# Pools that wait per tile, and three stages moved in a two-layer mixer, attention and FFN kernel (Trainium2, one core)

## The chip, the cores and the metric

The kernel runs on one core of a Trainium2 chip. The metric is the device time of one execution in microseconds (us). The engines are TensorE (PE, with PEld for its weight loads), VectorE (DVE), ScalarE (ACT), GpSimd (POOL) and SyncE (SP, which here only issues transfers).

## The reference

Two residual layers on x of 2048 positions by 1024 features, float32:

```
block 1:  h = x @ w_in;  y = concat(SGU(h), conv module(h), HGRN2(h)), each times silu(gate)
          x1 = layernorm(sqrt(2)*x + y @ w_out)
block 2:  n = rmsnorm(x1); y = concat(attention heads on n, a pooling mixer on n)
          x2 = x1 + y @ w_out2
          m = rmsnorm(x2);  x3 = x2 + (act(m @ w_gate) * (m @ w_up)) @ w_down
out = rmsnorm(x3)
```

The FFN is 1024 to 2816 to 1024. Positions are the rows; attention is causal.

## The kernel before

Every float32 operand is split into an fp16 high and an fp16 low part, and a product is three matmuls (high x high, high x low, low x high). The kernel runs its stages one after the other in the program, and a scheduler of the framework then sets, ahead of time, the order of the instructions of each engine; each engine works through its own list in that order. A transfer is issued by the engine in whose list it stands, almost always SP.

SBUF and PSUM are handed out by pools (`pool`, L71). A pool that is opened where an earlier one has been closed lies in its space, and the first write into the new pool waits until all tiles of the old pool that it lies on are released, pool against pool.

- **Block 1** ends with `out_phase` (L550): the mixers' output y lies in a DRAM scratch y1d, written by `store` (L194) as 512-position rows, loaded for 256 positions at a time (L567), multiplied by w_out, normalized, transposed by DMA.
- **Block 2** (`block2`, L705) runs six attention units, each in four blocks of 512 positions, in pools named E (10 tiles, `e`), U and others. Scores are matmuls into `sc` (L831), the exponentials are cast on POOL and ACT (L844, L845), transposed by DMA on SP (`e<-e`, L847) and multiplied with v (`po`, L868). `store` writes each unit's output to the scratch y2d. The pooling mixer runs between attention rows.
- **Second projection** (`out2`, L621): opens after block 2's pools close. One pool `gen` of eight 4 KB buffers (per partition) holds three of the eight w_out2 row weights (made on ACT, L120, and POOL, L121; the other five go to the always open pool W) and the y tiles: four tiles of 256 positions are needed for a pair of steps, and five buffers are left for them. For eight steps u of 2 x 128 positions: y loads (L650), x1 load (L657), 2 x 2 groups of 24 matmuls into `pq` (L663 to L665), the add (L666), the store of x2 (L667), Square (L671), scaling (L673), seven sums for a Strassen-like product (`seven`), fp16 splits (L680, L681), and DMA transposes on SP (L692, 11 for a step) into T7 tiles in the pools x7 and T (`th`, `tl`).
- **FFN, first part** (`ffn_in`, L1079): 22 blocks of 128 hidden features in pairs, each for two halves of the positions. A product is 7 sub-products of 12 matmuls (L1102 to L1104). Each pair's weights come by `seven_weights` (L1056, L1057 loads into the two-buffer pool WS; L1063 to L1066 on POOL; L1069 casts on ACT; L1070 low parts on DVE or POOL). The hidden values go to a DRAM scratch `md` (L1153).
- **FFN, second part** (`ffn_out`, L1157): opens its own pools `wd`, `gwt`, `gm`, `gs`, `gsm` where `ffn_in`'s have closed, loads all eight x2 rows (L1168), makes three sets of w_down weights (a set is two loads, four POOL operations, three ACT casts, three DVE subtractions), and multiplies the `mid` tiles (L1240) with them (L1190 to L1192), in four chunks of 3, 3, 3 and 2 pairs; the accumulation goes back into the x2 rows (L1184, L1198, L1200), and `finish` normalizes and stores.

Of the kernel before, what the change touches and what calls it, by code (L numbers as in the profile page):

```python
# [7 lines left out]
F32 = mybir.dt.float32  # L8
F16 = mybir.dt.float16
# [9 lines left out]
D = 1024  # L19
# [47 lines left out]
class Kernel:  # L67
# [3 lines left out]
    def pool(self, name, bufs=1, space=None, ctx=None):  # L71
        kw = {"space": space} if space is not None else {}
        return (ctx or self.ctx).enter_context(self.tc.tile_pool(name=name, bufs=bufs, **kw))
# [115 lines left out]
    def y_scratch(self, name):  # L189
        return [  # L190
            [self.dram.tile([128, KD, 512], F16, name=f"{name}{b}{p}") for p in "hl"] for b in range(NB)
        ]

    def store(self, yd, k, b, src, scale=None):  # L194
# [10 lines left out]
        nc.sync.dma_start(yd[b][0][:, k], yh)  # L205
        nc.sync.dma_start(yd[b][1][:, k], yl)
# [336 lines left out]
    def out_phase(self, cw, blk):  # L543
# [19 lines left out]
        for b in range(NT // 2):  # L563
            y = []
            for p in range(2):
                t = yp.tile([128, KD, 256], F16, tag=f"y{p}", name="y")
                nc.sync.dma_start(t, yd[b // 2][p][:, :, (b % 2) * 256:(b % 2 + 1) * 256])  # L567
                y.append(t)
            yh, yl = y
            for c in range(2):  # L570
                t = b * 2 + c
                cs, ts = slice(c * 128, (c + 1) * 128), slice(t * 128, (t + 1) * 128)
# [8 lines left out]
                for n in range(2):  # L581
                    ns = slice(n * 512, (n + 1) * 512)
                    ps = pq()
                    for k in range(KD):
                        wh, wl = w[k]
                        nc.tensor.matmul(ps, yh[:, k, cs], wh[:, ns], start=k == 0, stop=False)
                        nc.tensor.matmul(ps, yh[:, k, cs], wl[:, ns], start=False, stop=False)
                        nc.tensor.matmul(ps, yl[:, k, cs], wh[:, ns], start=False, stop=k == KD - 1)
# [33 lines left out]
    def out2(self, cw):  # L622
# [20 lines left out]
        for u in range(4 * NB // 2):  # L643
            half, tp = u // 4, u % 4
            if tp % 2 == 0:
                ys = []
                for q in range(2):
                    for p in range(2):
                        t = gen.tile([128, KD, 256], F16, tag="w", name="y")
                        nc.sync.dma_start(t, self.y2d[2 * half + q][p][:, :, tp * 128:tp * 128 + 256])  # L650
                        ys.append(t)
            xs = []
            cs = slice(tp % 2 * 128, tp % 2 * 128 + 128)
            for q in range(2):
                yh, yl = ys[2 * q:2 * q + 2]
                r = m.tile([128, D], F32, tag="x2", name="x2")
                nc.sync.dma_start(r, self.x1d[8 * half + 4 * q + tp])  # L657
                for n in range(2):
                    ns = slice(n * 512, (n + 1) * 512)
                    ps = pq()  # L660
                    for k in range(KD):
                        wh, wl = w[k]
                        nc.tensor.matmul(ps, yh[:, k, cs], wh[:, ns], start=k == 0, stop=False)  # L663
                        nc.tensor.matmul(ps, yh[:, k, cs], wl[:, ns], start=False, stop=False)  # L664
                        nc.tensor.matmul(ps, yl[:, k, cs], wh[:, ns], start=False, stop=k == KD - 1)  # L665
                    nc.vector.tensor_tensor(r[:, ns], r[:, ns], ps, ALU.add)  # L666
                nc.sync.dma_start(self.x2d[u][:, q], r)  # L667
                xn = xp.tile([128, 2, 512], F32, tag="xn", name="xn")
                xf = xn.rearrange("p h n -> p (h n)")
                ss = sm.tile([128, 1], F32, tag="ss", name="ss")  # L670
# [670 lines left out]
```

## Time and profile before

| what | value |
|---|---|
| median of 3 runs (lowest to highest) | 3462.16 us (3456.29 to 3462.77) |
| profiled execution, its own time | 3461.33 us |
| its span in the trace | 3459.5 us |
| PE busy | 3128.8 us (90%), 17736 matmuls |
| DVE busy | 2270.6 us (66%) |
| POOL busy | 1337.9 us (39%) |
| ACT busy | 1217.1 us (35%) |

PE is the engine that is busiest throughout. A stretch in which its busy time or its granted clock (PEclk, 1.00 being full speed, 2.4 GHz) is low is one in which it waits or has just waited. In time order: block 1 to 957 us, attention to 1968, second projection 1978 to 2177, FFN first part to 3003, second part to the end.

### The profile page before, as it was taken

Reading aid. Unit: us, or ns where it says so; the run is one execution under the profiler, and the core shown is the slowest. Engines: PE = TensorE matmul, PEld = TensorE weight load, DVE = VectorE, ACT = ScalarE, POOL = GpSimd, SP = SyncE. Lnnn points to the kernel's source line nnn. Section 1 sums busy time; section 2 is a strip of 40 time slices with the busy share of each in tenths; the row PEclk is TensorE's granted clock in tenths of the full one; section 3 lists DMA queues with packets and bytes.
Section 4 is the critical chain, followed back from the end, with each engine's and each line's share of the span. In section 5 each row is a group of like instructions: output and inputs, shape, how many; then the busy total and the mean of one; then the engine's idle time right before and its main releaser. Section 6 shows DMA issues by size and latency. Waiting matters only on the chain. (4 is left out here: it accounts for less than half of the span.)

```text
span 3459.5 us, 46900 instructions
## 1 busy us (share of the span) xinstructions
PE 3128.8 (90%) x17736; PEld 1586.8 (46%) x17736; DVE 2270.6 (66%) x3661; ACT 1217.1 (35%) x2259; POOL 1337.9 (39%) x1181
## 2 busy tenths in 40 slices
PE   8999998999987799868789698999999999789998
PEld 4454454784444455434444343344444444334443
DVE  6986878525648888889785644555655656454436
ACT  5223232322234466644565522332322332221103
POOL 5344354404335544474553400333322232074325
PEclk9999999999998999989999798999999999899999
DMA  5101011216756666546545677422222222533334
GB/s 186 37 17 46 13 50 50 63 32 193 182 139 120 126 124 139 117 102 126 123 100 112 141 176 198 115 67 80 79 83 67 81 83 80 209 129 133 112 109 161
DMA packets 575106, 371.84 MB, mean 107 GB/s; under 512 B 434848, under 2 KB 524704, under 8 KB 573856
## 3 DMA queue, kind: packets, MB, share of 16 engines
q1 hardware_dynamic: 567360, 348.22, 38.9%
q10 hardware_dynamic: 7520, 20.63, 1.7%
q8 instruction: 139, 2.28, 0.3%
q14 instruction: 87, 0.71, 0.1%
HBM read 162.70 MB, written 82.31 MB: 71 GB/s over the span
## 5 line engine op out<-in xcount | busy, mean ns | idle before, releaser
L142 PE MATMUL pg<-th,w 128*128 128x512 f16 x1344 | 522.4, 389 | 39.3 <-DVE r L590 11.8
L144 PE MATMUL pg<-th,w 128*128 128x512 f16 x1344 | 522.2, 389 | 5.9 <-POOL w L155 3.0
L143 PE MATMUL pg<-tl,w 128*128 128x512 f16 x1344 | 522.6, 389 | 0.7 <-DVE tl L181 0.7
L868 PE MATMUL po<-v,e 128*128 128x128 f16 (+1 forms) x1088 | 170.6, 260 | 107.9 <-DMA e<-e 91.2
L980 POOL TENSOR_TENSOR e<-e 128x128 f32<-128x128 f32 (+7 forms) x96 | 165.1, 1723 | 193.7 <-DVE e L974 154.6
L845 POOL TENSOR_TENSOR e<-e 128x1024 f16<-128x1024 f32 (+4 forms) x96 | 154.8, 1627 | 196.5 <-ACT e L844 165.3
L844 ACT CAST e<-e 128x1024 f16<-128x1024 f32 (+7 forms) x192 | 150.4, 794 | 222.8 <-POOL e L967 98.0
L143 PEld LDWEIGHTS <-w 128*128 128x128 f16 x1344 | 134.4, 100 | 182.9 <-issue 46.3
L142 PEld LDWEIGHTS <-w 128*128 128x128 f16 x1344 | 134.5, 100 | 171.0 <-issue 17.5
L144 PEld LDWEIGHTS <-w 128*128 128x128 f16 x1344 | 134.1, 100 | 166.4 <-issue 15.5
L974 DVE TENSOR_TENSOR_SCAN e<-e,few 128x129 f32<-128x129 f32 (+7 forms) x96 | 185.4, 1936 | 34.7 <-POOL e L967 31.4
L1070 POOL TENSOR_TENSOR w<-ws,w 128x1024 f16<-128x1024 f32 x20 | 48.0, 2400 | 393.3 <-ACT w L1069 393.3
L831 PE MATMUL sc<-k,q 128*128 128x512 f16 (+2 forms) x480 | 173.8, 364 | 28.1 <-DVE e L894 22.2
L465 DVE SCALAR_TENSOR_TENSOR acc<-h,cols,acc 128x512 f32<-128x512 f32 x240 | 193.5, 826 | 2.4
L1103 PEld LDWEIGHTS <-w 128*128 128x128 f16 x1232 | 120.7, 98 | 161.6 <-issue 20.5
L1102 PEld LDWEIGHTS <-w 128*128 128x128 f16 x1232 | 120.7, 98 | 150.7 <-ACT w L1069 4.8
L1104 PEld LDWEIGHTS <-w 128*128 128x128 f16 x1232 | 120.7, 98 | 149.6 <-DVE w L1070 4.0
L899 ACT ACTIVATE e<-e,nm 128x1024 f32<-128x1024 f32 (+4 forms) x192 | 171.2, 893 | 51.0 <-DVE e L894 25.8
L832 PE MATMUL sc<-k,q 128*128 128x512 f16 (+2 forms) x480 | 172.2, 366 | 0.0
L868 PEld LDWEIGHTS <-e 128*128 128x128 f16 x1088 | 107.9, 104 | 136.9 <-issue 59.4
L869 PE MATMUL po<-v,e 128*128 128x64 f16 (+1 forms) x1088 | 163.8, 216 | 0.0
L121 POOL TENSOR_TENSOR w<-ws,w 128x1024 f16<-128x1024 f32 x52 | 117.9, 2270 | 113.3 <-ACT w L120 113.2
(317 smaller groups left out, 8000.2 us busy)
## 6 DMA issues: line engine op xcount, KB each, us to landing
mid<-md SPq DMA_DIRECT2D x88, 448.0 KB, 4.2
ws<-in_w SPq DMA_DIRECT2D x48, 512.0 KB, 3.8
md<-mid SPq DMA_DIRECT2D x44, 512.0 KB, 3.4
md<-mid SPq DMA_DIRECT2D x22, 768.0 KB, 5.7
q<-qn SPq DMA_DIRECT2D x96, 128.0 KB, 2.4
ws<-in_wg SPq DMA_DIRECT2D x22, 512.0 KB, 3.5
ws<-in_wu SPq DMA_DIRECT2D x22, 512.0 KB, 4.1
ws<-in_wd SPq DMA_DIRECT2D x22, 512.0 KB, 3.8
```

Of the source, the lines that this page charges most:

```text
L142: nc.tensor.matmul(ps, wh[:, k], th[:, k], start=k == 0, stop=False)
L143: nc.tensor.matmul(ps, wh[:, k], tl[:, k], start=False, stop=False)
L144: nc.tensor.matmul(ps, wl[:, k], th[:, k], start=False, stop=k == KD - 1)
L465: nc.vector.scalar_tensor_tensor(acc[:, ct], src, wcol, acc[:, ct], ALU.mult, ALU.add)
L831: nc.tensor.matmul(ps[:, 0:n], q[:, 0], kk, start=True, stop=False)
L832: nc.tensor.matmul(ps[:, 0:n], q[:, 1], kk, start=False, stop=not last)
L845: eng.tensor_tensor(fv[:, n:2 * n], A[:, 0:n], fv[:, 0:n], ALU.subtract)
L868: nc.tensor.matmul(po, t[:, 0, j], v, start=x == 0, stop=False)
L869: nc.tensor.matmul(po[:, 0], t[:, 1, j], v[:, 0], start=False, stop=x == len(todo) - 1)
L899: nc.scalar.activation(e[r][:, 0:n], e[r][:, 0:n], AF.Exp, bias=nm[:, len(sc) - 1:len(sc)], scale=-1.0, accum_out=ss[:, r, x:x + 1])
L974: nc.vector.tensor_tensor_scan(rev, rev, self.zero.to_broadcast([128, n + 1]), 1.0, ALU.mult, ALU.add)
L980: nc.gpsimd.tensor_tensor(A[:, 0:n], g[:, 1:n + 1], g[:, 0:n], ALU.subtract)
```

## The change

1. All SBUF and PSUM pools get `reuse_waits="tile"`: a tile of a new pool waits only for the tiles of the old pool that it lies on. A pool can be put on the right side of SBUF; x7 is.
2. The y scratches are laid out in blocks of 128 positions. A load of y is then one contiguous piece for each partition (4 KB in `out_phase`, 2 KB in `out2`; before, 512 B pieces), and a store is four pieces of 256 B for each partition (before, one of 1 KB).
3. `out2`: the w_out2 weights and the y tiles have pools of their own, `gen` with 3 buffers and `uy` with eight 2 KB buffers; y is loaded for 128 positions at a time (32 loads of 256 KB in place of 16 of 512 KB). The pools are opened in another order. The normalized row is written in place; Square goes by halves into a PSUM tile, and one more POOL addition joins the two sums (16 more instructions on ACT and on POOL in all). The x1 rows have 5 buffers instead of 2.
4. FFN: the pools for w_down's intermediate sums, `seven`'s sums and the mid tiles are opened once for both parts. The first three w_down sets are made in the last gate/up pair, between its gate and its up product. An x2 row is asked for one step ahead, instead of all eight at the start. The extra mid pool has one buffer, used in one turn of six (before two, in two turns of seven).

```diff
     def pool(self, name, bufs=1, space=None, ctx=None, side="left"):
         kw = {"space": space} if space is not None else {}
+        if space is not DRAM:
+            kw |= {"reuse_waits": "tile", "side": side}
...
-            [self.dram.tile([128, KD, 512], F16, name=f"{name}{b}{p}") for p in "hl"] for b in range(NB)
+            [self.dram.tile([128, 4, KD, 128], F16, name=f"{name}{b}{p}") for p in "hl"] for b in range(NB)
...
-        nc.sync.dma_start(yd[b][0][:, k], yh)
-        nc.sync.dma_start(yd[b][1][:, k], yl)
+        for p, t in enumerate((yh, yl)):
+            nc.sync.dma_start(yd[b][p][:, :, k], t.rearrange("p (c t) -> p c t", c=4))
...
-                t = yp.tile([128, KD, 256], F16, tag=f"y{p}", name="y")
-                nc.sync.dma_start(t, yd[b // 2][p][:, :, (b % 2) * 256:(b % 2 + 1) * 256])
+                t = yp.tile([128, 2, KD, 128], F16, tag=f"y{p}", name="y")
+                nc.sync.dma_start(t, yd[b // 2][p][:, b % 2 * 2:b % 2 * 2 + 2])
...
-        gen = self.pool("gen", 8, ctx=cw)
-        xp = self.pool("ux", 2, ctx=cw)
+        sm = self.pool("usm", 4, ctx=cw)
+        gen = self.pool("gen", 3, ctx=cw)
+        yp = self.pool("uy", 8, ctx=cw)
+        m = self.pool("um", 5, ctx=cw)
+        hp = self.pool("uh", 5, ctx=cw)
         sp = self.pool("us", 1, ctx=cw)
-        hp = self.pool("uh", 5, ctx=cw)
-        m = self.pool("um", 2, ctx=cw)
-        sm = self.pool("usm", 4, ctx=cw)
         pq = self.banks("upq", UPQ, cw)
+        jp = self.pool("ujk", 1, PSUM, ctx=cw)
...
-            if tp % 2 == 0:
-                ys = []
-                for q in range(2):
-                    for p in range(2):
-                        t = gen.tile([128, KD, 256], F16, tag="w", name="y")
-                        nc.sync.dma_start(t, self.y2d[2 * half + q][p][:, :, tp * 128:tp * 128 + 256])
-                        ys.append(t)
...
+                y = []
+                for p in range(2):
+                    t = yp.tile([128, KD, 128], F16, tag="y", name="y")
+                    nc.sync.dma_start(t, self.y2d[2 * half + q][p][:, tp])
+                    y.append(t)
...
+                    nc.vector.tensor_tensor(r[:, n], r[:, n], ps, ALU.add)
+                    junk = jp.tile([128, 512], F32, tag="junk", name="junk")
+                    nc.scalar.activation(junk, r[:, n], AF.Square, accum_out=ss[:, n:n + 1])
+                nc.sync.dma_start(self.x2d[u][:, q], rf)
+                nc.gpsimd.tensor_tensor(ss[:, 0:1], ss[:, 0:1], ss[:, 1:2], ALU.add)
+                self.rstd(ss[:, 0:1], ss[:, 0:1], self.eps_rms, 1.0 / D)
+                nc.vector.scalar_tensor_tensor(rf, rf, ss[:, 0:1], gr, ALU.mult, ALU.mult)
...
-            self.x7 = self.pool("x7", 6, ctx=c3)
+            self.x7 = self.pool("x7", 6, ctx=c3, side="right")
...
+            self.wt = self.pool("fwt", 1, ctx=cw)
+            self.sp = self.pool("fs", 1, ctx=cw)
+            self.mp = self.pool("gm", 1, ctx=cw)
+            self.sm = self.pool("gsm", 4, ctx=cw)
...
                     wg = weights(a["wg"], f + 2, 0, nc.gpsimd)
+                elif half:
+                    self.sets = [self.down_weights(j, 0, j) for j in range(CHUNKS[0])]
                 proj(wu, half, h, False)
...
-        for t in range(8):
+
+        def row(t):
             r = self.tp.tile([128, 2, D], F32, tag=("th", "tl")[t % 2], name="x2")
             nc.sync.dma_start(r, self.x2d[t])
             rows.append(r)
...
-        sets = [weights(j, 0, j) for j in range(CHUNKS[0])]
+        sets = self.sets
+        row(0)
...
-                    pool, tag = (mp, "m") if turn % 7 in (2, 5) else (self.wp, "w")
+                    pool, tag = (self.mp, "m") if turn % 6 == 1 else (self.wp, "w")
...
+                if len(rows) < 8:
+                    row(tp + 1)
```

`down_weights` is the old inner function `weights` of `ffn_out` made a method.

How the lists change at three places. The number of matmuls is the same, and block 1's lists are alike but for two ACT rows.

SP's list before, at the end of the attention (`e<-e` are the transposes of the exponentials, `ws<-in_wo` the last w_out2 row, y2d0 to y2d3 the scratch by 512 positions, h and l its high and low parts):

```order
L847 DMA_TRANSPOSE e<-e 128x14x128
L205 DMA y2d2h<-yh 128x512
L206 DMA y2d2l<-yl 128x512
L847 DMA_TRANSPOSE e<-e 128x16x128 x2
L132 DMA ws<-in_wo 128x1024
L650 DMA y<-y2d0h 128x8x256
L650 DMA y<-y2d0l 128x8x256
L650 DMA y<-y2d1h 128x8x256
L650 DMA y<-y2d1l 128x8x256
L657 DMA x_18882<-x1d_7493 128x1024
```

SP's list now, some twenty transfers earlier in the attention's end:

```order
L653 DMA y<-y2d0h 128x1024
L653 DMA y<-y2d0l 128x1024
L134 DMA ws<-in_wo 128x1024
L1061 DMA ws<-in_wg 128x1024
L848 DMA_TRANSPOSE e<-e 128x16x128
L848 DMA_TRANSPOSE e<-e 128x2x128
L848 DMA_TRANSPOSE e<-e 128x16x128
L848 DMA_TRANSPOSE e<-e 128x4x128
L848 DMA_TRANSPOSE e<-e 128x16x128
L848 DMA_TRANSPOSE e<-e 128x6x128
L208 DMA y2d1h<-yh 512x1x128
L653 DMA y<-y2d1h 128x1024
```

The first two y loads, the last w_out2 row and the first gate row, which stood behind the attention's last transposes, now stand ahead of fifteen of them. The first load of y2d1 stands right behind the store that it reads, and seven more y loads follow between transposes: ten of 256 KB in all ahead of the attention's last transpose.

PE's list before, at the same place (`po` is the attention's last product, `pt` a transpose of its result, `pq` the second projection):

```order
L868 LDWEIGHTS e
L868 MATMUL po<-v,e 128x256
L869 LDWEIGHTS e
L869 MATMUL po<-v,e 128x128
L876 MATMUL pt<-ident,o_18377 128x128 x4
L663 LDWEIGHTS y
L663 MATMUL pq<-w,y 128x512
L664 LDWEIGHTS y
```

PE's list now, at the last query block's scores (`sc`):

```order
L833 LDWEIGHTS q
L833 MATMUL sc<-k_17310,q 128x384
L835 LDWEIGHTS bias_8827
L835 MATMUL sc<-bias_8827 128x128
L665 LDWEIGHTS y
L665 MATMUL pq<-w,y 128x512
L666 LDWEIGHTS y
```

Two groups of the second projection (48 matmuls) now stand among the scores of the attention's last rows, and 44 more matmuls of it around the last `po` products: about 92 of 768 that were all behind the last `po`.

PE's list before, at the passage from the FFN's first part to its second (`pa`, `pb`, `pc` are the accumulators; `th`, `tl` and `x_` tiles hold the first part's input, `mid` the second's):

```order
L1103 LDWEIGHTS w_24931
L1103 MATMUL pa<-tl,w_24931 128x512
L1104 LDWEIGHTS w_24931
L1104 MATMUL pa<-th,w_24931 128x512
L1190 LDWEIGHTS mid
L1190 MATMUL pc<-wd,mid 128x512
L1191 LDWEIGHTS mid
L1191 MATMUL pc<-wd,mid 128x512
```

PE's list now:

```order
L1107 MATMUL pc<-th,w_25164 128x512
L1108 LDWEIGHTS w_25164
L1108 MATMUL pc<-x_18864,w_25164 128x512
L1197 LDWEIGHTS mid
L1197 MATMUL pb<-wd,mid 128x512
L1198 LDWEIGHTS mid
L1198 MATMUL pb<-wd,mid 128x512
L1199 LDWEIGHTS mid
```

The first products of the second part (L1197 to L1199 of the changed kernel) stand ahead of the last 72 matmuls of the first part. SP's list there, before (`md` is the scratch of the hidden values, `x_` from x2d the x2 rows):

```order
L1168 DMA x_25584<-x2d_18857 128x2048
L1240 DMA mid<-md_20146 128x1792
L1153 DMA md_20167<-mid 512x1x512 x2
L1153 DMA md_20167<-mid 512x1x768
L1240 DMA mid<-md_20148 128x1792 x2
L1056 DMA ws<-in_wd 128x1024
L1057 DMA ws<-in_wd 128x1024
L1056 DMA ws<-in_wd 128x1024
L1057 DMA ws<-in_wd 128x1024
```

and now:

```order
L1061 DMA ws<-in_wd 128x1024
L1062 DMA ws<-in_wd 128x1024
L1248 DMA mid<-md_20232 128x1792
L1159 DMA md_20249<-mid 512x1x512 x2
L1159 DMA md_20249<-mid 512x1x768
L1061 DMA ws<-in_wd 128x1024
L1062 DMA ws<-in_wd 128x1024
L1184 DMA x_25697<-x2d_18853 128x2048
L1061 DMA ws<-in_wd 128x1024
L1062 DMA ws<-in_wd 128x1024
L1184 DMA x_25840<-x2d_18855 128x2048
L1061 DMA ws<-in_wd 128x1024
```

The loads for sets 2 and 3 of w_down stood behind the last stores into `md`; all three sets' loads, and the first of set 4, now stand ahead of the last two groups of `md` stores.

## Rows read from the trace of the kernel before

**Rows 1.** Table of stretches: length, then each engine's busy time and count, PEclk, DMA share.

```profile
1860.00:1963.00 103.00, 77.46 (x465) 43.69 (x464) 82.76 (x223) 69.94 (x142) 47.77 (x31) 0.89 0.57 119
1963.00:1978.00 15.00, 5.99 (x35) 4.20 (x32) 3.29 (x2) 5.37 (x13) 8.45 (x6) 0.61 0.41 107
1978.00:2177.00 199.00, 176.79 (x771) 77.48 (x772) 90.26 (x106) 44.37 (x61) 11.78 (x31) 0.91 0.77 192
...
2950.00:3003.00 53.00, 51.09 (x236) 22.82 (x234) 28.30 (x42) 11.80 (x20) 0.00 (x0) 1.00 0.43 153
3003.00:3052.00 49.00, 18.43 (x59) 6.54 (x58) 20.98 (x20) 13.83 (x15) 22.30 (x14) 0.69 0.60 218
3052.00:3100.00 48.00, 43.30 (x191) 19.00 (x191) 29.30 (x32) 10.26 (x10) 38.20 (x22) 0.96 0.46 154
```

**Rows 2.** PE's waits, attention's end (1860 to 1978): total us, times, longest.

```profile
PE po L868 <- DMA e<-e: 14.8, 6, 5.0
PE sc L831 <- DVE e L894: 9.3, 11, 2.6
PE pt L876 <- DVE o L948: 8.5, 1, 8.5
```

**Rows 3.** Timelines of POOL and of SP's queue around the second projection's start.

```profile
1969.59 4.64 POOL L121 TENSOR_TENSOR w<-ws,w 128x1024 f16<-128x1024 f32 x2
...
1971.73 0.34 SPq L132 DMA_DIRECT2D ws<-in_wo  x1
1972.19 0.60 SPq L650 DMA_DIRECT2D y<-y2d0h  x1
```

**Rows 4.** PE's waits in the second projection (1978 to 2177).

```profile
PE pq L665 <- DMA y<-y2d2l: 16.0, 2, 8.2
PE pq L665 <- DMA y<-y2d0l: 5.9, 2, 4.5
```

**Rows 5.** Timeline of PE behind one of those waits.

```profile
2082.86 0.61 PE L665 MATMUL pq<-w,y 128*128 128x512 f16 x1 [8.22 <-DMA y<-y2d2l]
...
2086.67 0.63 PE L665 MATMUL pq<-w,y 128*128 128x512 f16 x1
2087.10 0.45 PE L663 MATMUL pq<-w,y 128*128 128x512 f16 x1
```

**Rows 6.** PE's waits at the FFN's middle (3003 to 3100).

```profile
PE pb L1190 <- ACT wd L1069: 13.4, 3, 8.8
PE pc L1190 <- DMA mid<-md: 12.1, 1, 12.1
PE pa L1190 <- DVE x L1184: 2.4, 1, 2.4
```

**Rows 7.** Timeline of POOL: the first three w_down sets.

```profile
2929.89 1.77 POOL L1063 TENSOR_TENSOR ws<-ws 128x512 f32<-128x512 f32 x1 [0.93 <-DVE u L1125]
...
3020.26 1.26 POOL L1064 TENSOR_TENSOR wt<-ws 128x512 f32<-128x512 f32 x1 [88.60 <-DMA md<-mid]
...
3029.05 1.27 POOL L1064 TENSOR_TENSOR wt<-ws 128x512 f32<-128x512 f32 x1
...
3039.13 2.12 POOL L1064 TENSOR_TENSOR wt<-ws 128x512 f32<-128x512 f32 x1 [1.75 <-DVE wd L1070]
```

**Rows 8.** Transfers: share by queue (1978 to 2177); landing and issue times by tile.

```profile
q1 hardware_dynamic: 72957, 37.62, 75.8%
...
L692 SPq DMA_TRANSPOSE tl<-hl x32: 1210/1257/2001, 2104.6 to 2192.7; - x32
...
DMA to landing us min/median/max: 1.9/2.0/5.4
```

**Rows 9.** SP's queue at the attention's end (1860 to 1972): its longest waits.

```profile
SPq L847 <- POOL e L845: 46.0, 12, 10.4
```

**Rows 10.** The page's costliest groups: the matmuls of block 2's first products among them.

```profile
L142 PE MATMUL pg<-th,w 128*128 128x512 f16 x1344 | 522.4, 389 | 39.3 <-DVE r L590 11.8
```

More of the change, by code (lines that the diff above doesn't have):

```diff
@@ L69, in __init__, with pool @@
         self.tc, self.nc, self.a, self.out, self.ctx = tc, tc.nc, a, out, ctx
-    def pool(self, name, bufs=1, space=None, ctx=None):
+    def pool(self, name, bufs=1, space=None, ctx=None, side="left"):
         kw = {"space": space} if space is not None else {}
+        if space is not DRAM:
+            kw |= {"reuse_waits": "tile", "side": side}
         return (ctx or self.ctx).enter_context(self.tc.tile_pool(name=name, bufs=bufs, **kw))
@@ L1057, in seven_weights @@
         nc.sync.dma_start(r2, b2)
-        t = wt.tile([128, 3, 512], F32, tag="wt", name="wt")
+        t = self.wt.tile([128, 3, 512], F32, tag="wt", name="wt")
         if inner:
@@ L1155, in ffn_in, with down_weights @@
                     )
+    def down_weights(self, f, c, j):
+        if c % 2:
+            h, lo = [self.wd[j].tile([128, 7, 512], F16, tag=p, name="wd") for p in "hl"]
+        else:
+            h, lo = [self.x7.tile([128, 7, 512], F16, tag="x7", name="wd") for _ in range(2)]
+        pools = [(h[:, s], lo[:, s]) for s in (slice(0, 2), slice(2, 4), slice(4, 7))]
+        wd = self.a["wd"]
+        src = [wd[(2 * f + x) * 128:(2 * f + x + 1) * 128].rearrange("p (h n) -> p h n", h=2) for x in range(2)]
+        return self.seven_weights(*src, False, pools, self.nc.vector)
     def ffn_out(self, cw):
         nc, a = self.nc, self.a
-        wd = [self.pool(f"wd{j}", 1, ctx=cw) for j in range(max(CHUNKS))]
-        wt = self.pool("gwt", 1, ctx=cw)
-        mp = self.pool("gm", 2, ctx=cw)
-        sp = self.pool("gs", 1, ctx=cw)
-        sm = self.pool("gsm", 4, ctx=cw)
-        fg = self.bcast(sp, a["final_g"], D, "fg")
+        self.wd = [self.pool(f"wd{j}", 1, ctx=cw) for j in range(max(CHUNKS))]
+        sp, sm = self.sp, self.sm
+        fg = self.bcast(sp, a["final_g"], D, "s3")
         rows = []
-        for t in range(8):
+        def row(t):
             r = self.tp.tile([128, 2, D], F32, tag=("th", "tl")[t % 2], name="x2")
@@ L1169, in ffn_out @@
             rows.append(r)
-        def weights(f, c, j):
-            if c % 2:
-                h, lo = [wd[j].tile([128, 7, 512], F16, tag=p, name="wd") for p in "hl"]
-            else:
-                h, lo = [self.x7.tile([128, 7, 512], F16, tag="x7", name="wd") for _ in range(2)]
-            pools = [(h[:, s], lo[:, s]) for s in (slice(0, 2), slice(2, 4), slice(4, 7))]
-            src = [a["wd"][(2 * f + x) * 128:(2 * f + x + 1) * 128].rearrange("p (h n) -> p h n", h=2) for x in range(2)]
-            return self.seven_weights(*src, False, wt, pools, nc.vector)
         def down(pairs, tp):
@@ L1233, in ffn_out @@
                 if tp == 1 and c + 1 < len(CHUNKS):
-                    nxt = [weights(at + n + j, c + 1, j) for j in range(CHUNKS[c + 1])]
+                    nxt = [self.down_weights(at + n + j, c + 1, j) for j in range(CHUNKS[c + 1])]
                 pairs = []
```

44 lines of the change are left out of this document (18 added, 26 removed).

## The prediction, made before the changed kernel had run

> **What bounds the kernel now.** I first read the table of stretches [rows 1], asking in which of them PE stands still or runs at a low granted clock, and then, for those alone, PE's waits, the timelines around them, and the transfers. Where nothing disturbs it PE sets the pace: from 2950 to 3003 it is busy for 51.09 of 53 us with 236 matmuls at PEclk 1.00, that is 0.2165 us each. Against this unit four places fall off. At the end of the attention (1860 to 1963) PE is busy for 77.46 of 103 us. Between attention and second projection (1963 to 1978) it is busy for 5.99 of 15 at PEclk 0.61. In the second projection 771 matmuls take 199 us where they would need 771 x 0.2165 = 167: 32 us lost. In the middle of the FFN, 59 matmuls take 49 us and then 191 take 48: (49 - 12.8) + (48 - 41.4) = 43 us lost. The change touches just these places.
>
> **The wait between attention and second projection.** The end of a chain is seen in [rows 3]: POOL makes row weights of the second projection at 1969.59, which need space of `gen` and so the end of the attention's pools; the last weight load can go out only at 1971.73 and the first y load follows at 1972.19. PE's wait for the attention's last result (8.5 us for `pt`, [rows 2]) lies in the same stretch, but the second projection doesn't need the last query block to begin. With a wait per tile and the y loads ten transfers ahead of the attention's last transposes, PE finds ready groups there. What PE does do in the stretch is worth 5.99 x 0.61 = 3.7 us at full clock, so 15 - 3.7 = **11 us** go. Bounds: 0, if the space that the new pools lie on is released last, to 11.
>
> **Groups moved into the attention's end.** About 92 of the 768 matmuls stand earlier in PE's list: 92 x 0.2165 = 20 us. PE's idle time in the attention's end is 14.8 us for transposed exponentials and 9.3 us for DVE's exponent work [rows 2], 24 us together, so there is room. Against it: ten y loads stand on SP ahead of exponent transposes, at 0.60 us for an issue [rows 3] 6 us of queue; behind them wait the transposes, and PE's `po` for those. SP itself waits 46.0 us for POOL's casts there [rows 9], so I take half of it as hidden: 20 - 3 = **17 us**. Bounds: 20, if all is hidden, to -5, if the groups stand in PE's list before their y has landed and hold the last scores behind them, for one wait like the 5.0 us of [rows 2], while gaining nothing.
>
> **Waits for y in the second projection.** PE waits 16.0 us for y2d2 low and 5.9 for y2d0 low [rows 4]; behind each wait matmuls are 0.43 us apart (2086.67 to 2087.10) instead of 0.2165, and only then does the clock return [rows 5]. 22 us of waits and 10 of low clock make the 32. The cause is space: a pair of steps needs four y tiles of 4 KB and only five buffers are left beside three weights, so the next pair's tiles can be asked for only when the last matmuls of this pair are done. Eight buffers of 128 positions hold two steps, and one step's buffers come free every 96 matmuls = 21 us, more than a landing. I leave 10 us for one wait with its low clock and take **22 us**. Bounds: 5, if transfers are what is late and not buffers (first rival), to 31.
>
> **Smaller pieces in stores, larger in loads.** Stores into y2d landed in 2.0 us at the median, in a row that counts eight stores and two loads of y2d2's low part together [rows 8]. The new first load of y2d1 stands right behind its store and needs it to have landed; two loads are so exposed, some 2 us each, within the 3 us above. Pieces of 256 B in a store aren't in this trace; as bounds I take no change and a doubling of the 2.0 us, 4 us for the two loads. The Trainium skill, "DMA: Bandwidth & Descriptors", Specifications, speaks against this edit: it asks for at least 512 B in a transfer for line rate, below which the DMA engine does a read-modify-write. By the trace the stores cost nothing visible; by that rule, with a doubling of the landing as an estimate, the sum would be 4 us smaller, 3380. No run here shows it yet.
>
> **Block 1 to block 2, and the added instructions.** PE waits 11.8 us for `r` before block 2's first product [rows 10]. A wait per tile frees one PSUM bank an add earlier, not the normalization that it waits for: **1 us**, bounds 0 to 4. The 16 extra instructions on ACT and on POOL lie in a stretch in which these are busy for 44.37 and 11.78 of 199 us [rows 1]: nothing. If that cover were gone, POOL's extra addition would stand in each row's chain of normalization, which ends in T7 and is not waited for until the FFN starts.
>
> **The middle of the FFN.** POOL's first sum for w_down waits 88.60 us, until 3020.26, for the last store of the hidden values, because its pool lies where the first part's pools were [rows 7]; the sets follow at 3029.05 and 3039.13, 9 to 10 us apart, and PE waits 13.4 us for ACT's casts and 12.1 for a `mid` tile that stands behind eight x2 rows [rows 6]. Now the sum's pool is the same in both parts, and all three sets are made in the last pair, during whose last half POOL is busy for 0.00, ACT for 11.80 and DVE for 28.30 of 53 us [rows 1]. Three sets, 9.4 us apart, are 28 us, and they can begin at 2929.89, where POOL already worked on the first [rows 7], 73 us before 3003. So they end in time. Of the 43 us I leave 9: 2.4 us for x2 adds [rows 6], which aren't touched, and half of the 12.1 for one late `mid` tile. Gain **34 us**; bounds 18 (the `mid` wait and its low clock stay in full and one set is late) to 42.
>
> **The sum.** 11 + 17 + 22 + 1 + 34 = 85 us. The profiled execution took 3461.33 us, 0.8 below the median of 3462.16, too little to matter: 3461.3 - 85 = **3376 us**.
>
> **The rivals.** *Transfers pace the second projection.* DMA's share is 0.77 over 199 us, the highest of these stretches, 153 us of work, nearly all in SP's queue [rows 1, 8]. My forecast leaves 199 - 22 - 20 = 157 us for the stretch; the ten loads moved ahead are 2.6 of its 37.62 MB, so 142 us of work would fill 0.91 of it. If no more than 0.77 is to be had, it takes 142 / 0.77 = 184 us, 27 more: **3403**. For it: 88 transposes at 1.257 us [rows 8] are 111 us of SP alone. Against it: the y loads' pieces are four times as long, which shortens their work. The Trainium skill, "Perfetto Trace Analysis", What "DMA-bound" means, would call it bound by the issuing engine's sequencer if SP's track were solid with transfers. Chance 0.20.
>
> *The moved groups gain nothing.* They fall where PE isn't idle, or what they fill is given back behind `po`: 17 less, **3393**. Chance 0.09.
>
> *The w_down sets are late in the last half.* If WS's two buffers, shared with the last gate and up weights, keep the loads back, PE waits in front of the first products, which now stand ahead of the last 72 matmuls of the first part: the gain is 12 instead of 34, **3398**. The longest wait for ACT's cast was 8.8 us [rows 6]. Chance 0.10.
>
> *Slower: the y loads hold SP's queue.* A load waits on SP for its buffer's space in E and U, and all transposes of exponentials wait behind it, then `po`, then the release of the next E tile. SP's longest wait of this kind was 10.4 us [rows 9]. At 10.4 us for each of ten loads it is 104 us, 3376 + 104 = **3480**. It decides from 85 / 10 = 8.5 us for a load. Against it: the pools now wait for single tiles, and the list puts the loads between transposes, where E tiles come free one by one. Chance 0.11, of which 0.03 end near 3461, where the change would also be seen to do nothing.
>
> *All at its best bounds.* 11 + 20 + 31 + 4 + 42 = 108: **3353**. Chance 0.06.
>
> **How the numbers follow.** That leaves 0.44 for the forecast, whose own range is 3364 to 3390. The range for 8 in 10 goes from 3348, just under the best bounds, to 3425, the first and third rivals together (27 + 22 more); outside lie the slower case and a little at the lower end. Faster by over 0.2% (7 us, about what a measurement of this kernel can tell from no change): 0.44 + 0.20 + 0.09 + 0.10 + 0.06 = 0.89; within 0.03; slower 0.08.
>
> **What would show it.** First two steps: `pq` matmuls inside the attention's end, no stretch of PEclk 0.6 behind the last `po`, PE's waits for `e<-e` no longer than 14.8 us. Third: no wait of PE for y, and the second projection ending near 2127 instead of 2177; if it ends near 2154 with DMA near 0.77 and waits for y, the first rival holds. FFN: POOL's 88.60 us wait gone, its w_down sums before the end of the first part, and 250 matmuls in about 65 us where there were 97. It would be wrong if PE waited for y or transposes among the last scores, or for w_down before the last 72 matmuls.

## The result, and the profile after

The changed kernel takes 3414.74 us (median of 4 runs, 3411.95 to 3417.88) against 3462.47 of the kernel before in the same comparison: ratio 0.9867, 95% interval 0.9849 to 0.9884. That is 47.7 us less; the forecast was 86 less (3376). The time lies in the range 3348 to 3425, but not in the 3364 to 3390 that the prediction gave to its own forecast. The profiled execution took 3417.88 us, its span is 3416.1.

The table of stretches of the changed kernel, in the same stretches as [rows 1] (length, then busy time and count of PE, PEld, DVE, ACT and POOL, PEclk, DMA share, GB/s):

```profile
1860.00:1963.00 103.00, 86.95 (x519) 46.27 (x517) 85.01 (x219) 70.75 (x140) 56.52 (x34) 0.97 0.69 148
1963.00:1978.00 15.00, 10.98 (x88) 7.09 (x88) 3.08 (x5) 2.36 (x10) 3.76 (x4) 1.00 1.03 272
1978.00:2177.00 199.00, 169.36 (x748) 73.85 (x747) 102.32 (x118) 61.10 (x107) 36.94 (x57) 0.92 0.76 187
...
2950.00:3003.00 53.00, 44.14 (x180) 18.67 (x180) 42.37 (x48) 18.39 (x26) 15.65 (x10) 0.91 0.73 264
3003.00:3052.00 49.00, 43.51 (x187) 18.76 (x185) 28.26 (x26) 8.28 (x9) 31.74 (x18) 0.93 0.52 185
3052.00:3100.00 48.00, 48.00 (x225) 21.72 (x222) 15.12 (x22) 2.35 (x4) 14.32 (x8) 1.00 0.28 98
```

Three stretches look as forecast. PE is busy for 86.95 of 103 us in the attention's end instead of 77.46, and for 10.98 of 15 behind it at PEclk 1.00 instead of 5.99 at 0.61. In the middle of the FFN it does 187 matmuls in 49 us instead of 59. But the stretch from 1978 to 2177 still shows PEclk 0.92 with fewer matmuls than before. PE's waits from 1860 to 2200 in the changed kernel (total us, times, longest) say why, set against [rows 2, 4]:

```profile
PE pa L1106 <- ACT junk L670: 17.4, 1, 17.4
PE po L869 <- DMA e<-e: 8.2, 7, 2.5
PE sc L832 <- DVE e L895: 6.0, 10, 2.0
PE pa L1106 <- ACT s L1121: 4.5, 1, 4.5
PE pc L1106 <- ACT w L1074: 2.7, 1, 2.7
PE pq L665 <- DMA y<-y2d2h: 2.0, 2, 1.7
```

The waits for y are down from 22 to some 4 us, those for transposed exponentials from 14.8 to 8.2. A wait that didn't exist has come: 17.4 us before the FFN's first matmul, and 4.5 and 2.7 right behind it. How far ahead of the kernel before the changed kernel is, is best seen where the same matmul starts in both traces (numbers counted within each part, us in the two spans):

| matmul | before | changed | ahead |
|---|---|---|---|
| second projection, last of 768 | 2176.3 | 2122.3 | 54.0 |
| FFN first part, 49th | 2199.3 | 2167.8 | 31.5 |
| FFN first part, 3547th of 3696 | 2965.7 | 2934.3 | 31.5 |
| FFN second part, 49th of 1848 | 3043.1 | 2988.6 | 54.5 |
| FFN second part, 301st | 3108.7 | 3057.9 | 50.8 |
| FFN second part, last | 3450.0 | 3405.6 | 44.5 |

So the second projection ended 54.0 us earlier, about what the first terms say (11 + 17 + 22 + 1). The FFN's start gave 22.5 back. Its middle brought 23.0, and the second part lost 10.0 of that on the way.

Who holds PE at the FFN's start? Rows of DVE, PE and SP in the changed kernel behind the last `pq` matmul at 2122.3 (L674 is the scaling, L668 the addition that empties a `pq` bank):

```profile
2124.98 1.28 DVE L674 SCALAR_TENSOR_TENSOR x<-x,ss,ws 128x1024 f32<-128x1024 f32 x1 [8.66 <-DMA x2d<-x]
...
2138.57 0.68 DVE L668 TENSOR_TENSOR x<-x,pq 128x512 f32<-128x512 f32 x1
2146.42 2.53 DVE L674 SCALAR_TENSOR_TENSOR x<-x,ss,ws 128x1024 f32<-128x1024 f32 x2 [7.17 <-DMA x2d<-x]
...
2140.11 0.58 PE L1106 MATMUL pa<-x,w 128*128 128x512 f16 x1 [17.44 <-ACT junk L670]
...
2150.14 0.53 SPq L1062 DMA_DIRECT2D ws<-in_wg  x1
```

Until 2124.98 the scaling waits 8.66 us for `x2d<-x`, the store of the raw row, because it now overwrites that row in place. The last addition comes at 2138.57, 16 us behind the last `pq` matmul, PE's first FFN matmul at 2140.11 behind it, the last scalings at 2146.42, and only behind them the second load of the first gate row (2150.14), whose WS buffer held the broadcast norm weight. DVE's waits from 1970 to 2170 in the changed kernel:

```profile
DVE x L674 <- DMA x2d<-x: 55.7, 10, 10.0
DVE hl L682 <- DMA x<-hl: 13.9, 7, 3.3
```

55.7 us for the raw rows' stores: the kernel before has no such wait in the same part, since there the normalized row had a tile of its own.

### The profile page after: what moved, and what is told of

The parts are those of the page before. It is cut to its first block, busy times and chain, and to the rows that moved or that the text cites. A ratio compares the mean times of both kernels' runs of the same rounds, so it can differ in the third digit from the quotient of the medians.

```text
span 3416.1 us, 46957 instructions
## 1 busy us (share of the span) xinstructions
PE 3110.3 (91%) x17736; PEld 1576.9 (46%) x17736; DVE 2274.2 (67%) x3661; ACT 1217.8 (36%) x2291; POOL 1357.9 (40%) x1197
## 5 line engine op out<-in xcount | busy, mean ns | idle before, releaser
L869 PE MATMUL po<-v,e 128*128 128x128 f16 (+1 forms) x1088 | 161.4, 252 | 98.6 <-DMA e<-e 85.3
L146 PEld LDWEIGHTS <-w 128*128 128x128 f16 x1344 | 133.7, 100 | 165.8 <-issue 13.5
L870 PE MATMUL po<-v,e 128*128 128x64 f16 (+1 forms) x1088 | 155.3, 211 | 0.0
```

Of the source, the lines that this page charges most:

```text
L146: nc.tensor.matmul(ps, wl[:, k], th[:, k], start=False, stop=k == KD - 1)
L869: nc.tensor.matmul(po, t[:, 0, j], v, start=x == 0, stop=False)
L870: nc.tensor.matmul(po[:, 0], t[:, 1, j], v[:, 0], start=False, stop=x == len(todo) - 1)
```

## The experiments

Most are the changed kernel with one edit; two put edits together, and one puts a part of the change into the kernel before. The first question is what holds the FFN's start: normalizing in place (theory A), the accumulator bank of the squares (B), the transfers of the second projection (C), or the norm weight's buffer (D).

**A tile of its own for the normalized row.**

```diff
+        xp = self.pool("ux", 2, ctx=cw)
-        m = self.pool("um", 5, ctx=cw)
+        m = self.pool("um", 3, ctx=cw)
...
-                nc.vector.scalar_tensor_tensor(rf, rf, ss[:, 0:1], gr, ALU.mult, ALU.mult)
-                xs.append(r)
+                xn = xp.tile([128, 2, 512], F32, tag="xn", name="xn")
+                xf = xn.rearrange("p h n -> p (h n)")
+                nc.vector.scalar_tensor_tensor(xf, rf, ss[:, 0:1], gr, ALU.mult, ALU.mult)
+                xs.append(xn)
```

> The changed kernel with the normalized row of the second projection in a tile of its own again (pool of two, x1 rows in three buffers instead of five). Theory A (the 17.4 us that PE waits before the FFN come from normalizing in place: VectorE's scaling has to wait until the store of the raw row has read it, 55.7 us in all, and the additions that free the accumulators queue behind it): those waits go, the first FFN matmul starts within 6 us of the last one of the second projection instead of 17.4, and the time is 3414.7 - 15 to 20 = about 3397 us. Rival B (the accumulator bank of the squares, opened where the FFN's first bank lies, is what holds PE): nothing changes, 3415. Rival C (transfers are late as such, the wait moves to the transposes or to the x1 rows, of which only three are held): 3408 to 3418.

Measured: 3417.5 us, ratio to before 0.9872 (0.9857 to 0.9886): no gain. Theory A in its simple form falls. DVE's waits and its scaling (duration min/median/max, first and last start) in this kernel:

```profile
DVE hl L685 <- DMA x<-hl: 15.4, 6, 7.9
DVE hl L685 <- issue: 14.6, 3, 11.1
...
DVE hl L685 <- DMA th<-hl: 11.6, 2, 9.3
...
L677 DVE SCALAR_TENSOR_TENSOR xn<-x,ss,ws x16: 1276/1284/1286, 1991.5 to 2152.7; 128x1024 f32<-128x1024 f32 x16
```

The wait for the store is gone, but DVE waits 27.0 us for the source tiles of the splits (`hl`), which the DMA transposes still read, and 14.6 more at the same instruction, for which the profile names nothing; the last scaling is at 2152.7 then, later than 2147.7. The second projection's last matmul came at 2142.4, with two waits for y of 8.3 and 7.7 us. This is the move that rival C had named. The edit also leaves three buffers for x1 rows instead of five, and DVE waits 7.7 us for an x1 row, so this run doesn't price the own tile by itself.

**The raw row's store issued by ScalarE.**

```diff
-                nc.sync.dma_start(self.x2d[u][:, q], rf)
+                nc.scalar.dma_start(self.x2d[u][:, q], rf)
```

> The changed kernel, still normalizing in place, with the store of the raw row issued by ScalarE instead of SyncE. Theory A, with the store late because it stands behind DMA transposes in SyncE's list: VectorE's waits for the store fall from 55.7 us to below 25 and the time to about 3400. Rival C (the transfer itself is slow, 4.4 us at the median): waits stay above 40 us, 3412 to 3418. Rival B: 3415.

Measured: 3420.44 us (0.9882, 0.9868 to 0.9897), no gain, if anything a little worse, and outside all three expectations. DVE's wait for the store in this kernel:

```profile
DVE x L674 <- DMA x2d<-x: 39.6, 10, 5.7
```

Less than 55.7, more than the 25 expected: standing behind transposes in SP's list was only a part of the store's lateness. What was won there went into a wait for y of 15.3 us.

**The norm weight in a buffer of its own.**

```diff
-        m = self.pool("um", 5, ctx=cw)
+        m = self.pool("um", 4, ctx=cw)
+        gp = self.pool("ugr", 1, ctx=cw)
...
-        gr = self.bcast(self.ws, a["n2"], D, "ws")
+        gr = self.bcast(gp, a["n2"], D, "gr")
```

> The changed kernel with the broadcast norm weight (the row `gr` that every scaling in the second projection reads) in a pool of its own instead of one of the two buffers of WS; x1 rows in four buffers instead of five. Theory D: the FFN's start hangs on the last scaling, since that row's buffer is what the second half of the first gate weights is loaded into (load at 2150.1, right behind the last scaling at 2147.7). Then the load moves ahead of the second projection's end, the FFN runs at full pace from its first matmul at 2140 on, and its 48th matmul comes at about 2150 instead of 2167.8: 3397 us. If PE is then held by ScalarE and VectorE, which still work off the last rows' splits (evictions queue behind them): 3407 to 3412. If the wait is only that for accumulators (17.4 us): 3415.

Measured: 3414.0 us (0.9863, 0.9848 to 0.9878), unchanged. Its last scaling, and PE's longest wait at the FFN's start:

```profile
L675 DVE SCALAR_TENSOR_TENSOR x<-x,ss,gr x16: 1279/1284/1286, 1989.3 to 2151.8; 128x1024 f32<-128x1024 f32 x16
...
PE pc L1107 <- ACT w L1075: 15.1, 1, 15.1
```

PE's wait now is for ScalarE's cast of the gate weights, which stands in ACT's list among the splits of the last rows. The weights' buffer was not the limit; the late rows are. Nor was the bank of the squares (B): here PE's first product goes to another bank (`pc`), and it starts no earlier (2143.4 against 2140.1).

**The low parts' transposes left out.**

```diff
                     for to, of in spots:
+                        if p:
+                            nc.gpsimd.tensor_copy(to, of)
+                            continue
                         nc.sync.dma_start_transpose(
```

> The changed kernel with the DMA transposes of the low parts in the second projection replaced by plain GpSimd copies of the same size, so the low parts are not transposed (that part of the computation is left out). SyncE issues 44 transposes less of 88. Theory C (transfers on SyncE's queue, 127 of 160 us busy behind the attention, pace what follows the matmuls, so that the last scaling comes 26 us after the last matmul): the last scaling follows the last matmul by less than 10 us, the 48th FFN matmul comes 15 to 20 us earlier than 2167.8, and the time is 3395 to 3400. Theory A (waits for the store's read) or the GpSimd copies being slow themselves: 3410 or more.

Measured: 3389.8 us (0.9792, 0.9777 to 0.9806), 25 us less than the changed kernel and below what theory C gave. My count of instructions was wrong: the low parts are half of the bytes, but 7 of a step's 11 transposes, so 56 of 88 went. The stretch 1970 to 2120, the scaling, and DVE's wait for the raw rows' stores in this kernel:

```profile
1970.00:2120.00 150.00, 147.69 (x697) 67.85 (x697) 92.80 (x106) 51.50 (x102) 64.40 (x97) 1.00 0.71 195
...
L674 DVE SCALAR_TENSOR_TENSOR x<-x,ss,ws x16: 1277/1286/1634, 1988.6 to 2123.9; 128x1024 f32<-128x1024 f32 x16
...
DVE x L674 <- DMA x2d<-x: 26.0, 8, 5.5
```

and the same stretch of the changed kernel:

```profile
1970.00:2120.00 150.00, 145.85 (x685) 66.42 (x686) 74.75 (x91) 43.86 (x90) 23.07 (x45) 1.00 0.84 208
```

The DMA share falls from 0.84 to 0.71, the waits for the stores from 55.7 to 26.0 us, and the last scaling follows the last matmul (2119.8) by 4 us instead of 25. PE's wait for the bank of the squares, which lies where it lay, is 1.6 us. The 49th FFN matmul came at 2141.8. So the transfers of the second projection hold the rows back, the raw rows' stores among them, and the rows hold the FFN's start. This is the prediction's first rival at another place: not PE's y waits, but what follows the matmuls.

**Fewer transposes, the same bytes.** The 14 parts go to other places in the seven tiles, so that each pair is one instruction: 64 transposes instead of 88.

```diff
-                    i = 7 * p + 2 * j
+                    i = 6 * p + 2 * j if j < 3 else 12 + p
...
-        i = 7 * p + q
+        i = 6 * p + q if q < 6 else 12 + p
```

> The changed kernel with the 14 parts of the normalized rows put into the seven tiles in another order, so that every transpose of two parts is one instruction: 64 DMA transposes in the second projection instead of 88, the same bytes, the result unchanged. If the issue of transposes on SyncE's queue (1.26 us each, whatever their size) is what paces the work behind the matmuls: 24 x 1.26 = 30 us of queue less, the 48th FFN matmul 12 to 20 us earlier than 2167.8, 3396 to 3403 us. If it is the bytes that the DMA engines move: 3412 to 3416.

Measured: 3398.09 us (0.9822, 0.9804 to 0.9839), 16.7 us less, inside what the issue theory gave, but not by its mechanism alone. Scaling, PE's wait at the FFN's start and DVE's wait for the stores:

```profile
L674 DVE SCALAR_TENSOR_TENSOR x<-x,ss,ws x16: 1276/1284/1285, 1982.7 to 2139.6; 128x1024 f32<-128x1024 f32 x16
...
PE pa L1106 <- ACT junk L670: 21.4, 1, 21.4
...
DVE x L674 <- DMA x2d<-x: 58.9, 13, 7.8
```

The last scaling is 8 us earlier (2139.6), the 49th FFN matmul at 2158.5, 9.4 earlier than in the changed kernel, where the issue theory gave 12 to 20. Of that 4.3 us were there before the attention began, where the two programs are the same. PE still waits 21.4 us and DVE 58.9 us for the stores. The rest of the gain lies in the FFN's middle: from the first part's 3547th matmul to the second part's 49th this kernel wins 30.6 us on the kernel before, the changed one 23.0, and the later loss of 10.0 is 3.7. The lists of the engines differ there too, since the parts lie in other tiles; I didn't separate that. (By the two traces the difference is 23 us, by the medians 16.7: the profiled executions took 3394.65 and 3417.88 us, on opposite sides of their medians.)

**All together.** First the fewer transposes with w_down's loads on ScalarE (that edit is tried alone below):

> The fewer transposes of the kernel before this one, and w_down's row loads issued by ScalarE (worth 5.5 us alone). The two lie 800 us apart and should add: 3391 to 3398 us; if the transposes' bytes pace, 3407 to 3410.

Measured: 3395.53 us (0.9809, 0.9793 to 0.9825), in the expected range but not the full sum: 2.6 us under the kernel with fewer transposes, where the 301st matmul of the second part had lost only 0.9 us on the 201st anyway (5.8 in the changed kernel). Then the normalized row's own tile on top of both:

> The kernel with 64 transposes and w_down's loads on ScalarE, and on top of these the normalized row in a tile of its own (two of these, x1 rows in three buffers). In the two runs before, PE still waited 21 us before the FFN with 24 transposes less on SyncE's queue, and VectorE's scalings still waited for the raw row's store. If those waits are what is left, the FFN's first matmul follows the last one of the second projection by less than 10 us instead of 21, and the time is 3381 to 3388. If the transfers as such pace, the waits move to the transposes' source tiles again, as they did when the own tile was tried alone: 3393 to 3400.

Measured: 3384.43 us (0.9778, 0.9762 to 0.9794), 11.1 us less, where the own tile alone had brought nothing. It is the fastest of all, and beats both kernels. Its scaling, PE's wait and the stretch 1970 to 2120:

```profile
L677 DVE SCALAR_TENSOR_TENSOR xn<-x,ss,ws x16: 1280/1285/1286, 1986.1 to 2132.0; 128x1024 f32<-128x1024 f32 x16
...
PE pa L1109 <- ACT junk L671: 10.7, 1, 10.7
...
1970.00:2120.00 150.00, 147.64 (x696) 67.47 (x694) 83.75 (x101) 47.86 (x96) 18.53 (x45) 1.00 0.93 224
```

The last scaling is 13.5 us earlier than without the own tile (2145.5), PE's wait 10.7 instead of 21.5, and DMA's share 0.93. So two waits stood one behind the other in the same loop, the store that the scaling overwrites and the transposes that free the split tiles: with either one relieved alone, the other stands (27.0 us for split tiles in the first run, 58.9 for stores with fewer transposes).

**Waits per pool again, all else as changed.**

```diff
-            kw |= {"reuse_waits": "tile", "side": side}
+            kw |= {"side": side}
```

> The changed kernel with waits per whole pool again; the order of every engine's list is the same. If the wait per tile is what lets the second projection begin in the attention's end: the moved groups hold PE until the attention's pools are released, at least the 11 and 17 us of the prediction are lost: 3440 or more. If the new places of the pools and the order do it alone: 3415 to 3420.

Measured: 3415.52 us (0.9869, 0.9854 to 0.9884): the same as the changed kernel. PE's longest wait from 1860 to 2200 is alike (16.0 against 17.4 us):

```profile
PE pa L1106 <- ACT junk L670: 16.0, 1, 16.0
```

The wait per tile, the first item of the change, is worth nothing here that this could show. What is left must do the work: the places and the sharing of the pools, the buffers, and the order of the lists. For the attention's end no run takes these apart.

**Four y buffers instead of eight.**

```diff
-        yp = self.pool("uy", 8, ctx=cw)
+        yp = self.pool("uy", 4, ctx=cw)
```

> The changed kernel with four y buffers of 128 positions instead of eight, so one step's tiles and none ahead. If buffers were what PE waited for before (as the prediction took it), waits for y come back, two to four of 4 to 8 us: the second projection's last matmul at 2135 to 2150 instead of 2122. Since the FFN's start was 36 us behind anyway, the time changes by less than that: 3415 to 3422. If transfers and not buffers set the loads: the same as the changed kernel everywhere, last matmul within 4 us of 2122.

Measured: 3446.16 us (0.9953, 0.9939 to 0.9968), 31.4 us more than the changed kernel, outside the expectation. The second projection's last matmul came at 2170.5, behind all that was expected. Rows of PE with two of its waits, and the scaling:

```profile
2036.06 0.61 PE L665 MATMUL pq<-w,y 128*128 128x512 f16 x1 [16.95 <-DMA y<-y2d0h]
...
2092.04 0.61 PE L665 MATMUL pq<-w,y 128*128 128x512 f16 x1 [12.34 <-DMA y<-y2d2h]
...
L674 DVE SCALAR_TENSOR_TENSOR x<-x,ss,ws x16: 1280/1284/1286, 1992.2 to 2176.6; 128x1024 f32<-128x1024 f32 x16
```

The waits for y are back, longer than before (16.95 and 12.34 us), so buffers were what PE lacked. They aren't all that it takes: in the first two experiments, with eight buffers, PE waited 16.0 and 15.3 us for y, whose loads had gone out late on SP. The time moved by more than I expected, because the last scaling came late too (2176.6): y loads that come late make the rows late, and the rows are what the FFN waits for.

**The FFN parts as before, and the FFN part alone.** Undone in the changed kernel (`ffn`, `ffn_in`, `ffn_out` and `seven_weights` of the kernel before):

> The changed kernel with both FFN parts as before (own pools, w_down sets after the first part, all x2 rows at the start), the waits per tile kept. From the difference of the two traces over the FFN's middle to the end (31.5 us ahead before it, 48.3 after) this part is worth 17 us: 3432. If it is worth the 34 us of the prediction, the rest being lost elsewhere: 3449. If the wait per tile alone already frees the sum's pool early: 3418 to 3424.

Measured: 3424.89 us (0.9893, 0.9877 to 0.991), so this part is worth 10.2 us there. PE's waits at the FFN's middle in this kernel answer [rows 6] almost one by one:

```profile
PE pc L1191 <- DMA mid<-md: 11.6, 1, 11.6
PE pb L1191 <- ACT wd L1070: 8.3, 3, 6.8
PE pb L1192 <- DVE wd L1071: 5.5, 3, 3.0
```

The time is near the 3418 to 3424 of the expectation's last case, but that case doesn't hold: POOL's wait for the last store of the hidden values is back, with waits per tile, so the change's FFN part took it away and not the wait per tile.

```profile
2986.95 1.26 POOL L1065 TENSOR_TENSOR wt<-ws 128x512 f32<-128x512 f32 x1 [86.69 <-DMA md<-mid]
```

And that part alone, put into the kernel before:

> The kernel before with the FFN part of the change alone (shared pools, w_down sets in the last gate/up pair, x2 rows one ahead). Taking this part out of the changed kernel cost 10.2 us, so if it is independent of the rest: 3463 - 10 = 3453 us. By the prediction's sum: 3429. If it needs the rest: 3460 or more.

Measured: 3445.17 us (0.9955, 0.994 to 0.997), 16.5 us less than before, between the 3453 and the 3429 of the expectation. In both kernels that have it, the FFN's middle brings 23 us up to the 49th matmul of the second part (23.0 and 22.9), and 10.0 or 6.7 us go again by the end.

**w_down's loads on ScalarE.** Rows of the FFN's middle in the changed kernel: POOL's first sum of the first and the third w_down set, two waits of PE, and SP's queue around the second wait:

```profile
2941.11 1.27 POOL L1069 TENSOR_TENSOR wt<-ws 128x512 f32<-128x512 f32 x1 [0.95 <-DMA ws<-in_wd]
...
2965.76 1.59 POOL L1069 TENSOR_TENSOR wt<-ws 128x512 f32<-128x512 f32 x1 [3.55 <-DVE wd L1075]
...
2994.17 0.59 PE L1197 MATMUL pb<-wd,mid 128*128 128x512 f16 x1 [4.09 <-DVE x L1191]
...
3042.65 0.61 PE L1197 MATMUL pa<-wd,mid 128*128 128x512 f16 x1 [4.22 <-DMA mid<-md]
...
3034.30 0.33 SPq L1061 DMA_DIRECT2D ws<-in_wd  x1
3035.53 0.33 SPq L1062 DMA_DIRECT2D ws<-in_wd  x1
3035.91 14.10 SPq L1248 DMA_DIRECT2D mid<-md  x6
```

The sets are made at 2941 to 2966, before the first part ends at 2988, as forecast, and the 88.60 us wait of [rows 7] is gone. But at 3042.65 PE waits 4.22 us for a `mid` tile whose load stood on SP behind w_down loads (3034.30, 3035.53) that waited for a WS buffer.

```diff
-    def seven_weights(self, b1, b2, inner, pools, eng):
+    def seven_weights(self, b1, b2, inner, pools, eng, q=None):
...
-        nc.sync.dma_start(r1, b1)
-        nc.sync.dma_start(r2, b2)
+        (q or nc.sync).dma_start(r1, b1)
+        (q or nc.sync).dma_start(r2, b2)
...
-        return self.seven_weights(*src, False, pools, self.nc.vector)
+        return self.seven_weights(*src, False, pools, self.nc.vector, self.nc.scalar)
```

> The changed kernel with w_down's row loads issued by ScalarE instead of SyncE. In the changed kernel a mid tile's load stands behind w_down loads that wait for a WS buffer (3034.3 to 3035.9), PE waits 4.2 us for it and runs slowly after it, 6 us in all. If that order on SyncE is the cause, the 300th to 400th matmul of the second part come 5 to 6 us earlier: 3409. If the mid tile's own buffer or the transfer is late: 3413 to 3416. If ScalarE, waiting to issue, delays its casts: 3418 or more.

Measured: 3409.22 us (0.9847, 0.9831 to 0.9863), 5.5 us less, as expected. PE's wait for `mid` and SP's row there:

```profile
PE pa L1197 <- DMA mid<-md: 0.5, 1, 0.5
...
3034.19 8.72 SPq L1248 DMA_DIRECT2D mid<-md  x6
```

The load goes out 1.7 us earlier (3034.19 instead of 3035.91), as soon as its buffer is free, and lands after 4.3 us instead of 6.7.

## Why the prediction was right, and where it wasn't

The sign and the range held; the gain was 48 us instead of 86. That the range held is in part luck: its upper end came from the first and the third rival, and what took the gain is a cost that neither describes. Step by step:

**The wait behind the attention, 11 us, and the moved groups, 17 us: right together.** 92 matmuls had started when the last `po` matmul did, as counted, and the clock didn't fall (PEclk 1.00 from 1963 to 1978). The last `po` was 5.1 us later than before, 1.9 of them there since block 2's first product, against the 3 that I took off. That the two terms are right follows from where the matmuls start; no run undoes them alone. The reason that I gave, waits for single tiles, was wrong: with waits per pool the time is the same.

**The waits for y, 22 us: right, and so was the cause.** Some 4 us are left, and with four buffers the waits return.

**Block 1 to block 2, 1 us: nothing.** Block 2's first product started 1.9 us later (996.3 against 994.4), not 1 earlier, within what differs between programs that are the same there (992.0 in the kernel with fewer transposes).

**Smaller store pieces: right.** The stores of y2d2's low part through the attention, before and after (count, size, median us to landing):

```profile
y2d2l<-yl SPq DMA_DIRECT2D x8, 128.0 KB, 1.9
```

```profile
y2d2l<-yl SPq DMA_DIRECT2D x8, 128.0 KB, 2.3
```

0.4 us more, where I had bounded it by 2.0. The rule of the Trainium skill ("DMA: Bandwidth & Descriptors", Specifications), at least 512 B in a transfer for line rate, goes the same way. Here the price is a fifth of a landing, and of what waits for it I found one wait of SP, 1.6 us, in front of the first load of y2d1.

**What follows the matmuls: the step that failed, 22.5 us.** I put the second projection's end where its last matmul is, and wrote of its normalization that it "is not waited for until the FFN starts". But the FFN's start was just what the gain moved forward. In the kernel before, the scaling ended with the matmuls:

```profile
L673 DVE SCALAR_TENSOR_TENSOR xn<-x,ss,ws x16: 1283/1285/1286, 1995.9 to 2179.6; 128x1024 f32<-128x1024 f32 x16
```

at 2179.6, 3 us behind the last matmul; PE's waits, as I read it, gave the rows time. In the changed kernel:

```profile
L674 DVE SCALAR_TENSOR_TENSOR x<-x,ss,ws x16: 1275/1284/1286, 1987.7 to 2147.7; 128x1024 f32<-128x1024 f32 x16
```

it is at 2147.7, 25 us behind. In both, the 49th FFN matmul comes 20 us after the last scaling (2199.3 and 2167.8), and in every kernel above 15 to 22 us after it. The rows' chain is paced by transfers, as leaving out 56 of the 88 transposes shows (25 us back). The edit that writes the normalized row in place I hadn't costed at all; undoing it alone brought nothing (with two x1 buffers less), with fewer transposes 11 us. The first rival had the right resource and nearly the right price (27 us), but I let it act through y loads and gave it 0.20. The nearness of the price is chance: it was worked out from a DMA share that can't exceed 0.77, and from 1970 to 2120 the changed kernel had 0.84.

**The FFN's middle, 34 us: mechanism right, size off.** It brought 23.0 by the second part's 49th matmul. The 9 us that I left were too few: PE waits 2.0 to 2.3 us three times in the first part's last half, where the additional work for w_down stands among the evictions. And 10.0 us went later: some 6 with the `mid` tile behind w_down's loads on SP (the run with these on ScalarE brought 5.5), the rest as waits for x2 additions up to the end, the first of them the 4.09 us at 2994.17. The order of PE's list had changed less than the lists in the section on the change suggest: by the traces 12 matmuls of the second part stood ahead of the first part's last one before, and 45 do now, the first of them ahead of its last 96, not 72. I had read SP's list only up to the first `mid` tiles.

Whether the issue of transposes or the DMA engines' work paces the rows isn't settled. With 24 transposes less, which shortens SP's queue alone (some 110 us of issuing from 1970 to 2130 instead of 126), PE's wait was 21.4 us, no shorter. That speaks against the queue alone, but a part of that wait was the raw rows' stores, as the own tile on top of it showed. Nor was the engines' share of 0.84 in the changed kernel a ceiling: the fastest kernel has 0.93. By the Trainium skill ("Perfetto Trace Analysis", What "DMA-bound" means) the sequencer would be the limit if its track were solid. It was not: 126 of 160 us. The longest of SP's waits between 1970 and 2165 in the changed kernel:

```profile
SPq L693 <- ACT hl L681: 21.8, 12, 4.1
```

The lists changed with the edit too, and transposes issued from a second queue weren't tried.

## What to carry to other kernels

When PE's waits in a stage are removed, ask where the work behind PE ends, not where PE ends: it had been keeping up only because PE waited, and the next stage starts from it. Read the last instruction of each engine in the stage, and what frees the buffers between them, before crediting the whole gain. And where two waits stand one behind the other in a loop, an experiment on one of them alone can show nothing: try both together before dropping either.

## What was not expected of the hardware

A DMA transpose in the second projection held SP's queue about as long at the median with eight blocks of 128 x 128 as with four. Two groups that are all of one size, four blocks in the changed kernel and eight with the parts packed (duration min/median/max in ns):

```profile
L693 SPq DMA_TRANSPOSE tl<-hl x32: 1188/1226/1793, 2082.1 to 2162.9; - x32
...
L693 SPq DMA_TRANSPOSE x<-hl x24: 1232/1280/4029, 1985.4 to 2057.2; - x24
```

Some of the larger ones took up to 4 us, so all transposes together went from 121.6 to 95.8 us of SP's queue, a little less of a gain than 24 x 1.26 us. Nor does the size never matter: the attention's transposes, of up to 16 blocks, have a median of 1612 ns.

A store of a raw row took 4.2 us at the median to land while the transposes ran (2.9 to 7.7), longer than the 1.28 us of the scaling that waited for it.
